# The attention's bias table by one product of rounded numbers, its operands stacked over 97 rows, and its product moved from the k projection to the v projection

## The chip, the cores and the metric

The kernel runs on one core of a Trainium2 chip. The metric is the device time of one launch in microseconds; lower is better. The median of three runs of the kernel before is 672.82 us (672.76 to 673.3).

## The reference, cut to what matters

One decoder block works on 512 tokens of width 1024. Its first half computes `q | k | v | p | g_attn | g_pool = h @ W_in`, a causal attention with 8 heads of 64, a pooling mixer, and a gated merge; its second half is a feed-forward block with a causal convolution. The change touches the additive bias of the attention's logits alone:

```
bias_t = rel_bias.T                                      # (8 heads, 32 buckets)
dist   = q_pos - k_pos
logit  = (q . k) * 64**-0.5 + bias_t[:, t5_bucket(dist)]
logit  = where(dist >= 0, logit, -inf)
prob   = softmax(logit)
```

The bias depends on the head and the distance only, so a table of 8 heads by 640 distances holds all of it. Distances below zero (the masked keys) are a 33rd bucket with the value -1e30.

## The kernel before, in words

All matrix products work on numbers split in two: `hi` is the value rounded to TensorE's short format (fp32r), by ScalarE's copy, and `lo` is the rest, by a VectorE subtraction. A product is then three fp32r matmuls (`mm3`: hi*hi, hi*lo, lo*hi). The order of TensorE, VectorE and ScalarE is the order in which the program is written (`manual_schedule`); the DMA queues of SyncE (loads of weights) and GpSimd take theirs in the written order as well.

The projections of q, k and v accumulate over 8 slices of the contraction into four PSUM banks of 128 tokens each. q and p (the pooling mixer's input) come first. k follows as a generator: `fill(kgen, us)` writes out as many pieces of it (three matmuls, counted as 0.65) as fit, and other steps are written between the fills. v does the same with `vgen`. PSUM has 8 banks, handed out in turn: k lies in the four banks that p left, and the next banks asked for are those that q left, freed one by one by q's norm (`head_norm`, VectorE, four instructions, one for each bank).

The steps that the prediction names, in the written order:

- `pooling(0)`, `pooling(1)`: VectorE sums windows of p, then a split.
- `head_norm(qps, qr, "q")`: frees q's four banks.
- `pooling(2)`: VectorE sums in a row, then ScalarE's rounding `pool_h` and VectorE's rest `pool_l`.
- `bias_table()`: for the 512 and the 128 last distances one float32 matmul of a 0/-1 matrix `hot` (33 buckets by distances) with the table `rel` (33 buckets by 8 heads) into the banks `fp_0`, `fp_1`; ScalarE copies the result to `f_0`, `f_1`; GpSimd's queue writes both to the DRAM buffer `fd`. As `fp` asks for two banks, it takes q's first two.
- `pool_proj(0)`, `pool_proj(1)`: three matmuls each into the banks `pw_0`, `pw_1`, then ScalarE's `pl_h` and VectorE's `pl_l`, which frees the bank.
- `head_sums(kps, "k")` and `head_norm(kps, kr, "k")`: squares on ScalarE, sums on VectorE, a power on GpSimd (`hr_k`), the norm on VectorE (`n_k`), which frees k's banks.
- `stacks`: transposes of q and k (`T_True`, `T_False`) and their splits into `Q`, `K1` and `kz`.
- `logits(h)`: GpSimd's queue reads row h of `fd` back, each partition shifted by one element (`trev`); TensorE computes the logits into banks `S`; VectorE adds `trev` to them and takes the minimum (line 454).
- Behind the attention, for j in 0 to 7, the branches: the products `B` (pool) and `A` (attention) with the weights `br`, whose parts are `hi_br` (ScalarE) and `lo_br` (VectorE).

`load_unit` puts a weight load on SyncE's queue in one of five buffers, `ahead` makes its hi and lo parts two units before they are needed.

Of the kernel before, what the change touches and what calls it, by code (L numbers as in the profile page):

```python
# [7 lines left out]
F32 = mybir.dt.float32  # L8
F32R = mybir.dt.float32r
AF = mybir.ActivationFunctionType  # L10
# [8 lines left out]
H = 8  # L19
# [4 lines left out]
NB = 32  # L24
EPS = 1e-6
WINDOWS = (2, 4, 8, 16)
BIG = 1e30
NF = 640
NG = 16
AW = D + 2  # L30
FIRST = 5.2
# [20 lines left out]
def block_kernel(tc, x, cvec, ada, wtok, wch, pool_w, wbr, wout, wup, wdn, pack, table, out):  # L52
    nc = tc.nc
# [3 lines left out]
    with ctx:  # L57
# [11 lines left out]
        def slot(name, dt=F32, w=512):  # L69
            return sp.tile([P, w], dt, tag="s", name=name)  # L70

        def bank(name):
            return psp.tile([P, 512], F32, tag="b", name=name)
# [11 lines left out]
        plan += [(wtok[8 + i], f"v{i}") for i in range(4)]  # L85
        plan += [(wch[i], f"gate{i}") for i in range(NG)]
        for j in range(8):
            if 8 + j >= NG:
                plan.append((wch[8 + j], f"gate{8 + j}"))
# [117 lines left out]

        fd = dpool.tile([H, NF], F32, name="fd")

        def bias_table():  # L210
            for i, (c0, n) in enumerate(((0, 512), (512, NF - 512))):
                fp = bank(f"fp_{i}")
                nc.tensor.matmul(fp[:H, :n], rb_[: NB + 1, :H], hot[i][: NB + 1, :n], start=True, stop=True)
                nc.scalar.activation(fsb[i][:H, :n], fp[:H, :n], AF.Copy)
                nc.gpsimd.dma_start(fd[:, c0 : c0 + n], fsb[i][:H, :n])

# [92 lines left out]
        for k in range(KT):  # L309
            i = k // 2  # L310
            if k % 2 == 0:
                pw, qw = ready.pop(f"p{i}"), ready.pop(f"q{i}")
            c0 = (k % 2) * 512
# [15 lines left out]
            mm3s([(qps[t], hh[k][:, tslice(t)], hl[k][:, tslice(t)], qw[0][:, ws], qw[1][:, ws])  # L329
                  for t in range(TT)], k == 0, k == KT - 1, late=1)  # L330

        hot = [slot("hot_0"), slot("hot_1")]
        rb_ = slot("rel")
        fsb = [slot("f_0"), slot("f_1")]
        nc.sync.dma_start(rb_[: NB + 1, :H], table[:, NF:])
        for i, (c0, n) in enumerate(((0, 512), (512, NF - 512))):
            nc.sync.dma_start(hot[i][: NB + 1, :n], table[:, c0 : c0 + n])

        def tok_proj(i, ps, name):
            for kk in range(4):  # L340
                w = unit(f"{name}{kk}")
                for s in range(2):
                    k = 2 * kk + s
                    for t in range(TT):
                        mm3(ps[t], hh[k][:, tslice(t)], hl[k][:, tslice(t)],
                            w[0][:, s * 512 : s * 512 + 512], w[1][:, s * 512 : s * 512 + 512],
                            k == 0, k == KT - 1)
                        yield 0.65

        def gate_proj(i, store, name):  # L350
            w = unit(name)
            ps = bank(f"{name}_ps")
            for k in range(KT):
                mm3(ps, w[0][:, tslice(k)], w[1][:, tslice(k)], hh[k], hl[k], k == 0, k == KT - 1)
                yield 0.65
            g = slot(name)
            nc.scalar.activation(g, ps, AF.Copy)
            store[i] = g

        def fill(gen, us):  # L360
            while us > 0:
                c = next(gen, None)
                if c is None:
                    return
                us -= c
# [15 lines left out]
        def head_norm(ps, rss, name):  # L381
            res = []
            for t in range(TT):
                o = slot(f"n_{name}_{t}")
                nc.vector.tensor_tensor(
                    o.rearrange("p (h d) -> p h d", d=64), ps[t].rearrange("p (h d) -> p h d", d=64),
                    rss[t].unsqueeze(2).to_broadcast([P, H, 64]), op=ALU.mult)
                res.append(o)
            return res
# [13 lines left out]
        def stacks(pr, isq):  # L403
            src, gain = (qn, qgn) if isq else (kn, col(C_KG))
            tp = bank(f"T_{pr}_{isq}")
            for t in range(TT):
                nc.tensor.transpose(tp[:, tslice(t)], src[t][:, tslice(pr)], ident)
            for e in range(2):
                h = 2 * pr + e
                a = slice(e * 64, e * 64 + 64)  # L410
                b = slice(64 - e * 64, 128 - e * 64)
                if isq:
                    q = slot(f"Q_{h}", F32R)
                    nc.scalar.activation(q[a], tp[a], AF.Copy, scale=gain[a])
                    nc.vector.scalar_tensor_tensor(
                        q[b], tp[a], gain[a], q[a].bitcast(F32), op0=ALU.mult, op1=ALU.subtract)
                    Q[h] = q
                else:
                    k1 = slot(f"K1_{h}", F32R)
                    k2 = kz[e, pr % 2]  # L420
                    for r in (a, b):
                        nc.scalar.activation(k1[r], tp[a], AF.Copy, scale=gain[a])
                    nc.vector.scalar_tensor_tensor(
                        k2[a], tp[a], gain[a], k1[a].bitcast(F32), op0=ALU.mult, op1=ALU.subtract)
                    K1[h], K2[h] = k1, k2
# [123 lines left out]
        kgen = tok_proj(1, kps, "k")  # L549
# [8 lines left out]
        pooling(1)  # L558
        fill(kgen, 4)
        qn = head_norm(qps, qr, "q")  # L560
        fill(kgen, 4)
        pooling(2)
        fill(kgen, 1)
        bias_table()
        fill(kgen, 1)
        for g in range(2):
            pool_proj(g)
        fill(kgen, 3)
# [8 lines left out]
        fill(vgen, 4)  # L577
        kn = head_norm(kps, kr, "k")
        fill(vgen, 1)
        stacks(0, True)  # L580
        fill(vgen, 2)
        stacks(1, True)
# [20 lines left out]
        def gate_stream():  # L603
            for i in range(NG):
                yield from gate_proj(i, gates, f"gate{i}")

        gg = gate_stream()
        fill(gg, FIRST)
        share = (NG * 5.2 - FIRST) / H
        for h in range(H):  # L610
# [346 lines left out]
def _bucket(d):  # L957
    if d < 16:
        return d
    return min(31, 16 + int(math.log(d / 16) / math.log(8.0) * 16))  # L960


def _layout(a):
    f = {k: np.asarray(v) for k, v in a.items()}
    one = lambda k: f[k][0]
    c = np.ascontiguousarray
    arr = {}
    arr["x"] = c(f["x"][0])
    arr["cvec"] = c(f["c"])
    unit = np.zeros((6, D, 1), np.float32)  # L970
    unit[[1, 4]] = 1.0
    arr["ada"] = c(np.concatenate(
        [one("ada_w").T, one("ada_b")[:, None], unit.reshape(6 * D, 1)], axis=1)).reshape(48, P, AW)
    w = one("w_in")
    tok = w[:, :2048].reshape(4, 2, P, 4, 512)
    arr["wtok"] = c(tok.transpose(3, 0, 2, 1, 4)).reshape(16, P, 1024)
    ch = lambda m, kt: m.reshape(kt, P, -1, P).transpose(2, 1, 0, 3)
    arr["wch"] = c(ch(w[:, 2048:], KT)).reshape(16, P, 1024)
    arr["pool_w"] = c(one("pool_w").transpose(1, 0, 2)).reshape(P, 512)
    wa, wb = ch(one("w_branch_attn"), 4), ch(one("w_branch_pool"), 4)  # L980
    arr["wbr"] = c(np.concatenate([wa, wb], axis=2)).reshape(8, P, 1024)
    tokm = lambda m: c(m.reshape(m.shape[0] // 256, 2, P, 2, 512).transpose(0, 3, 2, 1, 4)).reshape(-1, P, 1024)
    arr["wout"] = tokm(one("w_out"))
    up = ch(one("w_up"), KT).reshape(2, NP, P, 1024)
    arr["wup"] = c(up.transpose(1, 0, 2, 3)).reshape(2 * NP, P, 1024)
    dn = one("w_down").reshape(NP // 2, 2, P, 2, 512)
    blocks = np.stack([dn[:, 0, :, 0], dn[:, 0, :, 1], dn[:, 1, :, 1], dn[:, 1, :, 0]])
    blocks = np.concatenate([blocks, np.zeros((4, 2 * NU - NP // 2, P, 512), np.float32)], axis=1)
    arr["wdn"] = c(blocks.reshape(4, NU, 2, P, 512).transpose(0, 1, 3, 2, 4)).reshape(4, NU, P, 1024)
    cols = lambda v: v.reshape(-1, P).T  # L990
    qk = lambda k: np.concatenate([one(k), one(k)])[:, None]
    inv = np.zeros((P, 64), np.float32)
    for g, wd in enumerate(WINDOWS):
        inv[:, 16 * g : 16 * g + 16] = 1.0 / np.minimum(np.arange(16) + 1, wd)
    cw = one("conv_w").reshape(3, 2 * NP, P).transpose(2, 1, 0).reshape(P, -1)
    arr["pack"] = c(np.concatenate(
        [cols(one("norm1_g")), cols(one("norm2_g")), qk("q_norm_g"), qk("k_norm_g"),
         cols(one("pool_scale")), inv, np.eye(P, dtype=np.float32), cw, cols(one("conv_b"))], axis=1))
    hot = np.zeros((NB + 1, NF), np.float32)
    for i in range(NF):  # L1000
        hot[NB if i < 127 else _bucket(i - 127), i] = -1.0
    rb = np.concatenate([f["rel_bias"], np.full((1, H), -BIG, np.float32)], axis=0)
    arr["table"] = c(np.concatenate([hot, rb], axis=1))
    return arr


# [20 lines left out]
```

## Time and the profile before

| | |
|---|---|
| median of three runs | 672.82 us |
| the profiled execution's own time | 672.42 us |
| its span in the trace | 670.6 us |
| TensorE busy | 659.7 us (98%) |
| VectorE busy | 516.9 us (77%) |
| ScalarE busy | 331.7 us (49%) |
| mean granted clock of TensorE | 0.999 |

The span runs from the first to the last recorded instruction; the profiled execution's own time is 1.8 us longer, and 0.40 us below the median of the three runs. Times in the trace count from the span's start. Busy time is the time in which an engine has at least one instruction under way.

### The profile page before, as it was taken

The numbers are of one execution on the slowest core, as the hardware profiler recorded it, in microseconds if no ns is written. First come the engines' busy times: TensorE is split into PE (matmuls) and PEld (weight loads), VectorE is DVE, ScalarE is ACT, GpSimd is POOL, SyncE is SP. The second block draws the span as 40 slices with busy tenths as digits, with TensorE's granted clock in tenths as the row PEclk, the third lists the DMA queues.
The fourth block names the chain that finished last, engine by engine and source line by source line (L and its number), as shares of the span: only waits on it lengthen the run. The fifth ranks groups of instructions, "written<-read, shape, count | busy, mean of one in ns | idle before, by whom it ended". The sixth has DMA issues, their size and how long they took to land.

```text
span 670.6 us, 8750 instructions
## 1 busy us (share of the span) xinstructions
PE 659.7 (98%) x3090; PEld 549.5 (82%) x3090; DVE 516.9 (77%) x854; ACT 331.7 (49%) x532; POOL 93.3 (14%) x125
## 2 busy tenths in 40 slices
PE   6999999999999999999999999999999999999997
PEld 4788788888888887888998888888888888888885
DVE  5795776888878588867578878878787878878774
ACT  6554347756665556504653443425343344767431
POOL 3002140000000054703011111120110001001000
PEclk9999999999999999999999999999999999999999
DMA  8885231355443396693267675966935447767751
GB/s 307 294 349 186 90 128 64 114 173 190 153 145 106 103 201 217 223 351 131 95 220 253 223 247 195 307 229 215 309 127 188 162 153 148 271 224 263 254 179 58
DMA packets 41889, 131.48 MB, mean 196 GB/s; under 512 B 5379, under 2 KB 5548, under 8 KB 41846
## 3 DMA queue, kind: packets, MB, share of 16 engines
q1 hardware_dynamic: 35270, 109.82, 48.7%
q0 software_dynamic: 6576, 21.12, 9.5%
q8 instruction: 24, 0.39, 0.3%
q14 instruction: 19, 0.16, 0.1%
HBM read 115.16 MB, written 15.76 MB: 195 GB/s over the span
## 4 chain that ended last, share of the span: by engine, by line
PE 92%; DVE 2%; DMA 2%; ACT 2%; issue 1%; SPq 0%; DVEq 0%; ACTq 0%
PE u L129 12%; PE u L130 12%; PE u L128 12%; PE gate_ps L128 4%; PE gate_ps L130 4%; PE gate_ps L129 4%; PE X L893 3%; PE X L892 3%; PE X L894 3%; PE p L138 2%; PE o L130 2%; PE o L128 2%; PE q L138 2%; PE o L129 2%; PE O L495 2%; PE Y L893 1%
## 5 line engine op out<-in xcount | busy, mean ns | idle before, releaser
L128 PE MATMUL u<-h2h,hi_up 128*128 128x512 f32 (+1 forms) x384 | 142.7, 372 | 0.0
L129 PE MATMUL u<-h2l,hi_up 128*128 128x512 f32 (+1 forms) x384 | 142.6, 371 | 0.0
L130 PE MATMUL u<-h2h,lo_up 128*128 128x512 f32 (+1 forms) x384 | 142.6, 371 | 0.0
L128 PEld LDWEIGHTS u<-h2h,hi_up 128*128 128x128 f32 x384 | 72.4, 188 | 12.6
L129 PEld LDWEIGHTS u<-h2l,hi_up 128*128 128x128 f32 x384 | 72.4, 188 | 12.5
L130 PEld LDWEIGHTS u<-h2h,lo_up 128*128 128x128 f32 x384 | 72.4, 188 | 12.3
L191 DVE CUSTOM_DVE_ANT_0 raw_ada<-raw_ada,cbc 128x1026 f32<-128x1026 f32 x48 | 59.0, 1250 | 5.5 <-issue 2.7
L762 ACT ACTIVATE uv<-u,pk 128x512 f32<-128x512 f32 x22 | 17.2, 780 | 85.8 <-PE u L130 85.8
L119 DVE TENSOR_TENSOR lo_up<-raw_up,hi_up 128x1024 fp32r<-128x1024 f32 x44 | 52.0, 1219 | 4.8 <-ACT hi_up L109 4.8
L128 PE MATMUL gate_ps<-h_h,hi_gate 128*128 128x512 f32 x128 | 50.0, 391 | 0.0
L130 PE MATMUL gate_ps<-h_h,lo_gate 128*128 128x512 f32 x128 | 50.0, 390 | 0.0
L129 PE MATMUL gate_ps<-h_l,hi_gate 128*128 128x512 f32 x128 | 49.9, 390 | 0.0
L109 ACT ACTIVATE hi_up<-raw_up 128x1024 fp32r<-128x1024 f32 x44 | 44.2, 1048 | 4.3 <-PE u L129 4.3
L815 POOL DMA_DIRECT2D tsum_t<-b x44 | 23.8, 541 | 145.1 <-DVE b L810 139.0
L763 DVE SCALAR_TENSOR_TENSOR uv<-u,pk,uv 128x511 f32<-128x511 f32 x22 | 16.5, 749 | 34.2 <-ACT uv L762 34.2
L119 DVE TENSOR_TENSOR lo_t<-raw_t,hi_t 128x1024 fp32r<-128x1024 f32 (+1 forms) x24 | 26.7, 1133 | 9.6 <-ACT hi_t L109 9.6
L762 ACT ACTIVATE ug<-u,pk 128x512 f32<-128x512 f32 x22 | 17.0, 774 | 32.1 <-PE u L130 32.1
L109 ACT ACTIVATE hi_t<-raw_t 128x1024 fp32r<-128x1024 f32 (+1 forms) x24 | 23.7, 988 | 17.9 <-PE Y L894 8.8
L204 POOL TENSOR_TENSOR wo_l<-raw_wo,wo_h 128x512 fp32r<-128x512 f32 x16 | 25.6, 1620 | 20.7 <-ACT wo_h L203 20.7
L130 PEld LDWEIGHTS gate_ps<-h_h,lo_gate 128*128 128x128 f32 x128 | 24.0, 188 | 5.1
L128 PEld LDWEIGHTS gate_ps<-h_h,hi_gate 128*128 128x128 f32 x128 | 24.0, 188 | 4.6
L129 PEld LDWEIGHTS gate_ps<-h_l,hi_gate 128*128 128x128 f32 x128 | 24.0, 188 | 4.5
(253 smaller groups left out, 1507.4 us busy)
## 6 DMA issues: line engine op xcount, KB each, us to landing
raw_ada<-in_ada SPq DMA_DIRECT2D x48, 513.0 KB, 5.2
raw_up<-in_wup SPq DMA_DIRECT2D x44, 512.0 KB, 4.6
b<-in_wdn SPq DMA_DIRECT2D x44, 256.0 KB, 5.8
tsum_t<-b POOLq DMA_DIRECT2D x44, 256.0 KB, 2.9
raw_t<-tsum_t SPq DMA_DIRECT2D x20, 512.0 KB, 4.7
raw_gate<-in_wch SPq DMA_DIRECT2D x16, 512.0 KB, 3.4
raw_b<-in_wdn SPq DMA_DIRECT2D x15, 512.0 KB, 3.9
raw_br<-in_wbr SPq DMA_DIRECT2D x8, 512.0 KB, 4.3
```

The source lines that it names most:

```text
L109: nc.scalar.activation(hi, raw, AF.Copy)
L119: nc.vector.tensor_sub(lo, raw, hi.bitcast(F32))
L128: nc.tensor.matmul(ps, sh, mh, start=start, stop=False)
L129: nc.tensor.matmul(ps, sh, ml, start=False, stop=False)
L130: nc.tensor.matmul(ps, sl, mh, start=False, stop=stop)
L138: nc.tensor.matmul(ps, sl if i else sh, mh if i else ml, start=False, stop=stop and i != late)
L191: nc.vector.tensor_tensor_reduce(out=raw, in0=raw, in1=cbc, op0=ALU.mult, op1=ALU.add, scale=1.0, scalar=0.0, accum_out=acol[:, i : i + 1])
L204: (eng or nc.vector).tensor_sub(lo[:, :w], src, hi[:, :w].bitcast(F32))
L762: nc.scalar.activation(t, ps, AF.Identity, scale=cw(2), bias=col(C_CB + i))
L815: nc.gpsimd.dma_start(tsum[n, i][:, u * 512 : u * 512 + 512], b[nm])
L892: nc.tensor.matmul(ps, sh, mh, start=start, stop=False, skip_group_check=True)
L893: nc.tensor.matmul(ps, sh, ml, start=False, stop=False, skip_group_check=True)
```

## The change

The 0/-1 matrix and the table are stored twice, one below the other: rows 0 to 32 and rows 64 to 96, with zeros between (97 rows). The matrix is loaded as `hotr` and rounded to fp32r by VectorE (`hot`; 0 and -1 stay exact). The table is loaded as `rel`; ScalarE rounds all 97 rows to `rels`, then VectorE puts the rest of the rounding in rows 64 to 96. One fp32r matmul over 97 rows gives hi and lo part together. The operands are made behind q's norm, and `bias_table()` moves from between the fills of k to behind the norm of k, among the fills of v, just ahead of the first transposes.

```diff
+NT = 64 + NB + 1
...
         def bias_table():
             for i, (c0, n) in enumerate(((0, 512), (512, NF - 512))):
                 fp = bank(f"fp_{i}")
-                nc.tensor.matmul(fp[:H, :n], rb_[: NB + 1, :H], hot[i][: NB + 1, :n], start=True, stop=True)
+                nc.tensor.matmul(fp[:H, :n], rbs[:NT, :H], hot[i][:NT, :n], start=True, stop=True)
...
-        hot = [slot("hot_0"), slot("hot_1")]
+        hot = [slot("hot_0", F32R), slot("hot_1", F32R)]
+        hotr = [slot("hotr_0"), slot("hotr_1")]
+        rbs = slot("rels", F32R)
         rb_ = slot("rel")
         fsb = [slot("f_0"), slot("f_1")]
-        nc.sync.dma_start(rb_[: NB + 1, :H], table[:, NF:])
+        nc.sync.dma_start(rb_[:NT, :H], table[:, NF:])
         for i, (c0, n) in enumerate(((0, 512), (512, NF - 512))):
-            nc.sync.dma_start(hot[i][: NB + 1, :n], table[:, c0 : c0 + n])
+            nc.sync.dma_start(hotr[i][:NT, :n], table[:, c0 : c0 + n])
...
         qn = head_norm(qps, qr, "q")
+        nc.scalar.activation(rbs[:NT, :H], rb_[:NT, :H], AF.Copy)
+        nc.vector.tensor_sub(rbs[64:NT, :H], rb_[64:NT, :H], rbs[64:NT, :H].bitcast(F32))
+        for i, n in enumerate((512, NF - 512)):
+            nc.vector.tensor_copy(hot[i][:NT, :n], hotr[i][:NT, :n])
         fill(kgen, 4)
         pooling(2)
-        fill(kgen, 1)
-        bias_table()
-        fill(kgen, 1)
+        fill(kgen, 2)
...
         fill(vgen, 1)
+        bias_table()
         stacks(0, True)
...
-    arr["table"] = c(np.concatenate([hot, rb], axis=1))
+    tab = np.concatenate([hot, rb], axis=1)
+    arr["table"] = c(np.concatenate([tab, np.zeros((64 - NB - 1, NF + H), np.float32), tab], axis=0))
```

On TensorE the two products stood among the k projection's matmuls (a name's first number counts the bank, its last one the buffer):

```order
L129 MATMUL k_2_646<-lo_k2_655,h_5_h_439 128x512
L130 MATMUL k_2_646<-hi_k2_653,h_5_l_440 128x512
L213 MATMUL fp_0_793<-hot_0_588,rel_590 8x512
L213 MATMUL fp_1_797<-hot_1_589,rel_590 8x128
L128 MATMUL k_3_647<-hi_k2_653,h_5_h_439 128x512
L129 MATMUL k_3_647<-lo_k2_655,h_5_h_439 128x512
```

and now stand among those of v, ahead of the first transposes of q:

```order
L130 MATMUL v_1_878<-lo_v1_807,h_3_h_357 128x512
L131 MATMUL v_1_878<-hi_v1_805,h_3_l_358 128x512
L214 MATMUL fp_0_943<-hot_0_588,rels_592 8x512
L214 MATMUL fp_1_947<-hot_1_589,rels_592 8x128
L411 MATMUL T_0_True_951<-pk_104,n_q_0_737 128x128
L411 MATMUL T_0_True_951<-pk_104,n_q_1_739 128x128
L411 MATMUL T_0_True_951<-pk_104,n_q_2_741 128x128
```

The products left their place between two pieces of k, whose matmuls now follow each other, and moved 75 matmuls down. On VectorE, between the last norm of q and the rest of v's first weights, three instructions are new; before:

```order
L385 TENSOR_TENSOR n_q_2_738<-q_2_292,hr_q_2_635 128x512
L385 TENSOR_TENSOR n_q_3_740<-q_3_293,hr_q_3_642 128x512
L119 TENSOR_TENSOR lo_v0_752<-raw_v0_748,hi_v0_750 128x1024
L520 TENSOR_TENSOR pd_2_1_769<-pt_2_612 128x511
L521 COPY pd_2_1_769<-pt_2_612 128x1
```

and now:

```order
L389 TENSOR_TENSOR n_q_3_743<-q_3_293,hr_q_3_645 128x512
L566 TENSOR_TENSOR rels_592<-rel_593,rels_592 33x8
L568 CAST hot_0_588<-hotr_0_590 97x512
L568 CAST hot_1_589<-hotr_1_591 97x128
L120 TENSOR_TENSOR lo_v0_759<-raw_v0_755,hi_v0_757 128x1024
L524 TENSOR_TENSOR pd_2_1_776<-pt_2_615 128x511
L525 COPY pd_2_1_776<-pt_2_615 128x1
```

Everything behind them on VectorE keeps its order (`lo_v0` and then `pooling(2)` come next) and starts behind three more instructions. On ScalarE the two copies `f` left their place between the rounding `pool_h` and that of v's second weights `hi_v1`; before:

```order
L203 ACTIVATE pool_2_h_783<-pool_2_778 128x512
L214 ACTIVATE f_0_591<-fp_0_793 8x512
L214 ACTIVATE f_1_592<-fp_1_797 8x128
L109 ACTIVATE hi_v1_806<-raw_v1_804 128x1024
L536 ACTIVATE pl_0_h_817<-pw_0_813,pk_104 128x512
```

and now:

```order
L565 ACTIVATE rels_592<-rel_593 97x8
L110 ACTIVATE hi_v0_757<-raw_v0_755 128x1024
L204 ACTIVATE pool_2_h_790<-pool_2_785 128x512
L110 ACTIVATE hi_v1_805<-raw_v1_803 128x1024
L540 ACTIVATE pl_0_h_816<-pw_0_812,pk_104 128x512
```

So `hi_v1` follows `pool_h` directly, and the rounding `rels` is new ahead of `hi_v0`. The banks go round by two as well: `pw_0` and `pw_1` take q's first two banks in place of `fp`, v takes q's other two and then those of `pw_0` and `pw_1`, and `fp`, now asked for behind v, takes the first two banks of k.

## Rows read from the trace of the kernel before

**Rows 1.** The page, part 4: shares of the chain that ended last, by engine.

```profile
PE 92%; DVE 2%; DMA 2%; ACT 2%; issue 1%; SPq 0%; DVEq 0%; ACTq 0%
```

**Rows 2.** TensorE's waits, first and last of five: total, times, longest (us).

```profile
PE cb L230 <- ACT crow L150: 3.4, 1, 3.4
...
PE B L130 <- DVE lo_br L119: 0.5, 1, 0.5
```

**Rows 3.** Timeline of TensorE, 76 to 87: start, duration (us), engine, line, operation.

```profile
76.52 0.39 PE L130 MATMUL k<-hi_k,h_l 128*128 128x512 f32 x1
76.83 1.24 PE L213 MATMUL fp<-hot,rel 33*8 33x512 f32 x4
78.00 0.50 PE L128 MATMUL k<-hi_k,h_h 128*128 128x512 f32 x1
...
78.81 0.40 PE L128 MATMUL k<-hi_k,h_h 128*128 128x512 f32 x1
...
86.98 0.39 PE L128 MATMUL v<-hi_v,h_h 128*128 128x512 f32 x1
```

**Rows 4.** Weight loads (PEld) of the table's product, same columns, idle time in brackets.

```profile
76.83 0.09 PEld L213 LDWEIGHTS fp<-hot,rel 33*8 33x8 f32 x2 [0.35 <-DVE n_q L385]
```

**Rows 5.** The tile fp: minimum, median and longest duration (ns) of its matmuls.

```profile
L213 PE MATMUL fp<-hot,rel x4: 269/429/593, 76.8 to 77.8; 33*8 33x512 f32 x2, 33*8 33x128 f32 x2
```

**Rows 6.** Timeline of VectorE and ScalarE, 74 to 87.

```profile
74.60 2.48 DVE L385 TENSOR_TENSOR n_q<-q,hr_q 128x512 f32<-128x512 f32 x4
...
81.12 0.16 DVE L526 TENSOR_TENSOR fx<-pd,pk 128x8 f32<-128x8 f32 x1
...
81.52 0.63 ACT L203 ACTIVATE pool_h<-pool 128x512 fp32r<-128x512 f32 x1 [7.14 <-DVE pool L527]
...
82.06 0.73 ACT L214 ACTIVATE f<-fp 8x512 f32<-8x512 f32 x2
...
82.69 1.04 ACT L109 ACTIVATE hi_v<-raw_v 128x1024 fp32r<-128x1024 f32 x1
...
83.77 1.23 DVE L119 TENSOR_TENSOR lo_v<-raw_v,hi_v 128x1024 fp32r<-128x1024 f32 x1 [0.89 <-PE k L130]
...
84.91 1.40 DVE L537 SCALAR_TENSOR_TENSOR pl_l<-pw,pk,pl_h 128x512 fp32r<-128x512 f32 x2
...
85.57 0.74 DVE L537 SCALAR_TENSOR_TENSOR pl_l<-pw,pk,pl_h 128x512 fp32r<-128x512 f32 x1
```

**Rows 7.** VectorE's copy to fp32r, by form: count, busy us, mean ns, idle.

```profile
L107 DVE CAST hi_p<-raw_p 128x1024 fp32r<-128x1024 f32 x1 | 0.7, 689 | 0.0
```

**Rows 8.** Timeline of VectorE at 111: a short operation on one tensor.

```profile
111.19 0.29 DVE L468 TENSOR_SCALAR L<-L,ri 128x128 f32<-128x128 f32 x1
```

**Rows 9.** Timeline of VectorE and TensorE, 91 to 96.

```profile
91.72 1.87 DVE L385 TENSOR_TENSOR n_k<-k,hr_k 128x512 f32<-128x512 f32 x3
...
95.14 0.60 PE L407 MATMUL T_True<-pk,n_q 128*128 128x128 f32 x4
```

**Rows 10.** The tile f: issues of its writes to fd (ns), and their landing (us).

```profile
L215 POOL DMA_DIRECT2D fd<-f x2: 508/548/587, 82.9 to 83.5; - x2
...
DMA to landing us min/median/max: 1.5/1.7/1.9
```

**Rows 11.** The tile trev, 90 to 125: three reads of fd, issue to landing.

```profile
DMA to landing us min/median/max: 3.9/4.0/5.7
```

**Rows 12.** Timeline of VectorE at 107: the first use of trev.

```profile
107.77 0.69 DVE L454 CUSTOM_DVE_ANT_0 L<-S,trev 128x512 f32<-128x512 f32 x1
```

**Rows 13.** The chain that ended last, in order of time: two of its pieces.

```profile
229.31 0.60 ACT bot L502
...
240.68 8.61 DMA raw_ada<-in_ada
```

**Rows 14.** Timeline of TensorE at 263.

```profile
263.04 0.50 PE L130 MATMUL B<-pl_h,lo_br 128*128 128x512 f32 x1 [0.53 <-DVE lo_br L119]
```

**Rows 15.** The page, part 6: the loads of ada, KB each, median us to landing.

```profile
raw_ada<-in_ada SPq DMA_DIRECT2D x48, 513.0 KB, 5.2
```

## The prediction, as it was made before the run

> **What bounds the kernel now.** I read the page first, then TensorE's waits, then the timeline around the table's product, and last the rows of the other engines around the two places that the change touches. The chain that ended last lies on TensorE for 92% of the span [rows 1], and TensorE waits for another engine only five times in all [rows 2]. Four of those waits lie ahead of the projections or at their first matmuls; the fifth is 0.5 us in the branch stage, for VectorE's `lo_br`. From the projections on TensorE is a queue without gaps, apart from that one: a microsecond taken out of its work is one off the end, and a microsecond of new waiting is one on it. VectorE, ScalarE and the transfers count only where they make TensorE wait.
>
> In the timeline the regular step of TensorE is 0.227 us for a matmul of 512 columns: from 78.81 to 86.98 there are 36 of them in 8.17 us [rows 3].
>
> **What the change removes.** From the k matmul at 76.52 to the one at 78.81 there are four regular matmuls (0.91 us) and the table's product, in 2.29 us [rows 3]. So the float32 product costs 1.38 us in its old place. Of this its columns explain most: the four records differ by 593 - 269 = 324 ns for 384 columns more [rows 5], 0.84 ns for a column against 0.227 us / 512 = 0.44 for a regular one; twice 640 columns at 0.84 ns are 1.08 us. The other 0.30 us is a fixed price of the block: its first weights are loaded at 76.83 and not under the matmul ahead of it, with 0.35 us of idle time before [rows 4], and the regular matmul behind it takes 0.50 us instead of 0.39 and its followers come late [rows 3]. The idle time is put down to q's norm, but that is not what is waited for: the banks asked for are those of the first two of four `n_q`, and the whole row of four ends at 77.08 [rows 6], so the second was through by about 75.9. The whole 1.38 us therefore goes with the product.
>
> **What it adds on TensorE.** One fp32r pass over 640 columns is 640 x 0.44 ns = 0.28 us: that is the lower bound, if nothing else is paid. The upper bound has the 0.30 us of the old block once more: 0.58. The nearest row is the old product itself, which gives 8 rows of output as the new one does, so I take 0.58. The row that decides is [rows 4], where the small product's weights wait for the matmul ahead. The Trainium skill (TensorEngine Tiling (Array Packing), Key Properties) says that a change of the tiling mode, not only of the tile, drains TensorE; an output of 8 rows would be such a change in its old shape and in its new one, and the trace's 0.30 us for entering and leaving agrees with a drain that doesn't care for the number format. By that rule the new product costs the 0.58, without it the 0.28.
>
> **What it adds on VectorE, and who waits for it.** Three instructions now stand behind q's norm. The subtraction over 8 columns is like `fx`, 0.16 us [rows 6]. For the two copies to fp32r the trace has one of 1024 columns, 0.689 us [rows 7]; 640 columns in proportion are 0.43 us, the lower bound. The upper one takes a short operation's 0.29 us for 128 columns [rows 8] and a straight line from there to 0.689 for the 512: 0.46, together 0.75. So VectorE is later by 0.59 to 0.91 us; I take 0.75. ScalarE's rounding of 8 columns stands ahead of `hi_v0`, which VectorE needs only behind q's norm, so it is covered.
>
> What is queued behind is `lo_v0` and the whole of `pooling(2)`, then, through ScalarE, `hi_v1`, `lo_v1`, and the two `pl_l` that free the banks `pw_0` and `pw_1`. Before, ScalarE had `pool_h` at 81.52, the two copies `f` at 82.06 (0.73 us), and `hi_v1` from 82.69 for 1.04 us; `lo_v1` began 0.04 us behind its end, at 83.77 [rows 6]. (The row names a matmul of k as what ended that wait, but it ends with `hi_v1`.) Now the copies `f` are gone from there, and `hi_v1` follows `pool_h` directly: it begins at 82.06 + 0.75 = 82.81 instead of 82.69. Nearly all the VectorE time is covered by the 0.63 us that `f` held ScalarE, and `lo_v1` and what follows are 0.12 us later than before (-0.04 to +0.28 at the bounds).
>
> TensorE, though, comes 1.38 us earlier. The third bank of v is that of `pw_0`. v's first matmul into it is the 36th behind the one at 78.81 (three of k from there, six of `pw`, 21 of k, six of v); it stood at 86.98 [rows 3], and now at 85.60. The first `pl_l` ran from 84.91 for 0.74 us, to 85.65 [rows 6], now to 85.77. Before, the bank was free 1.33 us ahead of time; now it is 0.17 us late. With 0.04 us for the signal, and with a matmul behind a wait taking 0.50 instead of 0.39 us [rows 3, 14], TensorE loses 0.32 us here. At the lower bound the bank is free at 85.61, just when it is wanted, and I count nothing; at the upper one 0.48 us. I take 0.3. The second `pl_l`, 0.66 us later, meets a matmul that is 0.68 us later plus the same wait, and costs nothing more.
>
> **What moves at no cost.** The new place of the product asks for k's first two banks, the transposes `T_True` behind it for the third. Three `n_k` run from 91.72 for 1.87 us, to 93.59 [rows 9], now to about 93.7. TensorE was at the transposes at 95.14 [rows 9], so it comes to the product at 95.14 - 1.38 + 0.32 = 94.08: 0.37 us behind even the third norm. If that cover went, each microsecond of `n_k` would be one on the end. The writes to `fd` move with the product: it ends at 94.66, ScalarE's copies take 0.73 us, the two issues 1.1 us and the landing 1.9 us at most [rows 6, 10], so `fd` is there at about 98.4; the first `trev` takes up to 5.7 us [rows 11], to 104.1. VectorE adds it at 107.77 [rows 12], now about 0.5 us earlier, so about 3 us are left. Behind the writes on GpSimd's queue stand only the reads `trev`. The table's load grows from 33 to 97 partitions on SyncE's queue at 50 us, ahead of v's weights and of others that are used 20 us later; its cover is these 20 us.
>
> **The sum.** -1.38 + 0.58 + 0.30 = -0.50 us. Against the profiled execution's own time that is 672.42 - 0.50 = 671.92 us; the median of the runs stands 0.40 us above that execution, so I predict 672.3 us. By the bounds the gain is 0.32 to 1.10 us, 672.5 to 671.7 us. What a measurement of this kernel can tell from no change is about 0.2%, or 1.35 us: even the best case is within it.
>
> **The rivals.** *No wait at v's third bank.* If VectorE's three instructions cost their lower bound or hide better, nothing is lost there, and the gain is 0.8 us (with the product at 0.58) to 1.10 us (at 0.28): 671.7 to 672.0 us. For it: 0.17 us is less than I know the copies' time to. Against: the bank would still come at the very moment it is wanted.
>
> *The gain is given back in the branch stage.* From 229.31 on the chain that ended last leaves TensorE for ScalarE, VectorE and one transfer of `ada` of 8.61 us [rows 13], and returns with TensorE's wait of 0.53 us at 263.04 [rows 14]. There TensorE has no reserve. If the end of that chain is set by the transfers and not by TensorE's last attention product at 229.31, TensorE comes 0.5 us earlier and waits 0.5 us longer: 672.8 us. For it: a wait that exists already. Against it: the chain starts from a TensorE matmul, so it ought to move along.
>
> *Slower.* At that same place the load of `ada` that took 8.61 us, where the median of 48 is 5.2 [rows 15], lands later still, because it now meets the other transfers at another moment. Each microsecond there is one on the end. The kernel is slower than before from 0.5 us more, and by over 0.2% from 1.9 us more (10.5 us in all). The load has already spread by 8.61 - 5.2 = 3.4 us to the slow side; half as much again, 1.7 us, gives 674.0 us, the whole of it once more 675.7. Against it: the order of the loads is unchanged and they move together.
>
> **How the numbers follow.** My forecast has 0.55, no wait at v 0.20, the gain given back 0.11, slower 0.06; 0.08 is left for a gain of more than 1.35 us, which no row here supports. The range takes the bounds of the sum (671.7 to 672.5), the case that gives all back (672.8), and 0.2 us on either side for the spread of the three runs (672.76 to 673.3): 671.6 to 673.0 us. Faster by over 0.2%: 0.08; within: 0.86; slower by over 0.2%: 0.06.
>
> **What the profile after would show.** The k matmuls run on at 76.7 us in steps of 0.227. Two matmul records of the table stand at about 94, 0.28 us of columns and about 0.3 us around them. TensorE's list of waits has a new entry, v behind `pl_l`, of about 0.2 us at 85.6; if it is missing, the first rival holds. VectorE has 0.6 to 0.9 us of new work behind `n_q`, and `hi_v1` directly behind `pool_h`. The wait for `lo_br` near 262.5 stays at about 0.5 us; at 1 us the gain was given back there, at 2.5 us or more the kernel is slower. The prediction would be wrong, beyond these, if `trev` landed later than about 107, or if the product had to wait for k's norm at 94.

## The result: slower by 3.87 us, where 0.5 us less was predicted

The changed kernel takes 676.66 us (median of four runs, 676.18 to 677.0) against 672.79 us for the kernel before in the same runs: a ratio of 1.0055, 95% interval 1.0043 to 1.0066. The prediction (672.3 us, range 671.6 to 673.0) is wrong in sign and size. The profiled execution took 676.18 us, its span is 674.4 us, the granted clock 0.999 as before.

The page, part 4, of the changed kernel, answers to [rows 1]. TensorE's share of the chain that ended last is down from 92 to 83%; VectorE has 6% where it had 2, and transfers 4% where they had 2:

```profile
PE 83%; DVE 6%; DMA 4%; ACT 3%; issue 2%; SPq 1%; POOL 0%; DVEq 0%; ACTq 0%
```

TensorE's waits after (total, times, longest in us), the answer to [rows 2]; four others, ahead of the projections or at their first matmuls, are left out:

```profile
PE v L129 <- DVE pl_l L541: 2.7, 1, 2.7
...
PE k L130 <- DVE lo_k L120: 0.8, 1, 0.8
...
PE k L129 <- ACT hi_k L110: 0.4, 1, 0.4
PE B L131 <- DVE lo_br L120: 0.4, 1, 0.4
```

Three of these are new. One, v behind `pl_l`, was forecast at 0.2 us; it is 2.7. Two stand in k, of which the prediction says that it runs on without a gap. The wait for `lo_br` is 0.4 where it was 0.5. The same three in TensorE's timeline after (start, duration in us, engine, line, operation; idle time before it in brackets), with the new product; this answers to [rows 3, 9]:

```profile
77.47 0.39 PE L131 MATMUL k<-hi_k,h_l 128*128 128x512 f32 x1
78.27 0.50 PE L129 MATMUL k<-hi_k,h_h 128*128 128x512 f32 x1 [0.41 <-ACT hi_k L110]
79.53 0.50 PE L130 MATMUL k<-lo_k,h_h 128*128 128x512 f32 x1 [0.76 <-DVE lo_k L120]
...
87.52 0.39 PE L131 MATMUL v<-hi_v,h_l 128*128 128x512 f32 x1
90.65 0.50 PE L129 MATMUL v<-hi_v,h_h 128*128 128x512 f32 x1 [2.74 <-DVE pl_l L541]
...
98.73 0.39 PE L131 MATMUL v<-hi_v,h_l 128*128 128x512 f32 x1
98.95 0.45 PE L214 MATMUL fp<-hot,rels 97*8 97x512 f32 x2
99.24 0.60 PE L411 MATMUL T_True<-pk,n_q 128*128 128x128 f32 x4
```

Measured by the distance of two starts less the regular 0.227, the two waits in k cost 0.57 and 1.03 us, the slow steps behind them 0.28, and the wait in v 2.90 with 0.14 behind it: 4.92 us. From the first matmul of k to the first of the gate projection the kernel took 49.62 us before,

```profile
61.10 0.39 PE L128 MATMUL k<-hi_k,h_h 128*128 128x512 f32 x1
...
110.72 0.39 PE L128 MATMUL gate_ps<-h_h,hi_gate 128*128 128x512 f32 x1
```

and 53.43 after, 3.81 more:

```profile
61.38 0.39 PE L129 MATMUL k<-hi_k,h_h 128*128 128x512 f32 x1
...
114.81 0.39 PE L129 MATMUL gate_ps<-h_h,hi_gate 128*128 128x512 f32 x1
```

The old product's 1.38 us went and the new one's 0.29 came: 4.92 - 1.38 + 0.29 = 3.83. So the whole loss lies in this stretch, and it is waiting.

What is late? The chain that ended last, after, in order of time (start, duration in us, what):

```profile
54.97 5.11 SPq L78
...
61.42 8.30 DMA pwr<-in_pool_w
...
89.93 0.67 DVE pl_l L541
90.65 0.50 PE v L129
```

Ahead of v's late matmul it doesn't lie on TensorE. It runs through SyncE's queue, where the issue of v's weights (line 78) is on the path, through the load of the pooling weights `pwr` and ScalarE's rounding `pwh` into VectorE's work, which reaches TensorE as `pl_l`. The timeline of SyncE's queue, before:

```profile
50.49 0.72 SPq L337 DMA_DIRECT2D hot<-in_table  x2
51.31 3.43 SPq L77 DMA_DIRECT2D raw_v<-in_wtok  x3
54.80 0.43 SPq L552 DMA_DIRECT2D pwr<-in_pool_w  x1
```

and after:

```profile
50.68 3.48 SPq L341 DMA_DIRECT2D hotr<-in_table  x2
54.26 7.11 SPq L78 DMA_DIRECT2D raw_v<-in_wtok  x3
61.42 0.52 SPq L556 DMA_DIRECT2D pwr<-in_pool_w  x1
```

The two issues of the table take 3.48 us in place of 0.72, the three of v's weights 7.11 in place of 3.43. `pwr` is issued 6.6 us later, and lands 8.3 us behind its issue where it took 5.8. What the transfers did meanwhile is read from windows of one microsecond (the last two columns are the mean busy share of the 16 DMA engines and GB/s), before:

```profile
54.00:55.00 1.00, 1.00 (x7) 0.81 (x6) 0.46 (x2) 0.00 (x0) 0.00 (x0) 1.00 1.04 352
```

and after:

```profile
54.00:55.00 1.00, 1.00 (x6) 0.84 (x5) 0.96 (x2) 0.00 (x0) 0.00 (x0) 1.00 0.07 25
...
57.00:58.00 1.00, 1.00 (x7) 0.81 (x6) 0.00 (x0) 0.00 (x0) 0.00 (x0) 1.00 0.07 27
```

0.07 of sixteen engines is one engine, at 25 to 27 GB/s (so in five of the six windows from 54 to 60). The matrix of 97 x 640 numbers of 4 bytes is 248 KB, some 9.5 us at that rate, and the queue's next transfers stand behind it. The records of single packets in the trace, which no view above prints, show the same: the 97 rows of 512 columns (2048 bytes each) go one at a time, 0.08 us apart, from 54.08 to 61.82, and with the table's other two parts the load lasts from 53.5 to 64.7 us, 11.2 us, where the 33 rows took 1.7 us before. ScalarE at `pwh` shows the result: it sat idle for 5.84 us, and the rounding begins at 69.74, where it began at 63.50 before.

```profile
69.74 0.63 ACT L558 ACTIVATE pwh<-pwr 128x512 fp32r<-128x512 f32 x1 [5.84 <-DMA pwr<-in_pool_w]
```

From `pwl` at 70.41 VectorE works almost without a gap through the pooling, k's `lo_k`, q's norm (from 79.39; 74.60 before, [rows 6]) and the new copies to `pl_l`: 4.8 us late at q's norm, and 4.9 at the first `pl_l`.

### The profile page after: what moved, and what is told of

The parts are those of the page before. It is cut to its first block, busy times and chain, and to the rows that moved or that the text cites. A ratio compares the mean times of both kernels' runs of the same rounds, so it can differ in the third digit from the quotient of the medians.

```text
span 674.4 us, 8751 instructions
## 1 busy us (share of the span) xinstructions
PE 659.5 (98%) x3088; PEld 549.0 (81%) x3088; DVE 517.5 (77%) x857; ACT 331.5 (49%) x533; POOL 93.1 (14%) x125
## 4 chain that ended last, share of the span: by engine, by line
PE 83%; DVE 6%; DMA 4%; ACT 3%; issue 2%; SPq 1%; POOL 0%; DVEq 0%; ACTq 0%
PE u L131 12%; PE u L130 12%; PE u L129 12%; PE gate_ps L131 4%; PE gate_ps L130 4%; PE gate_ps L129 4%; PE X L900 3%; PE X L901 3%; PE X L899 3%; PE o L129 2%; PE o L131 2%; PE o L130 2%; DVE raw_ada L192 2%; PE O L499 2%; PE Y L900 1%
```

## The experiments

Three theories of the loss. **A:** the 97 rows go through one DMA engine, 97 being a prime number, and `pool_w`, behind them on the queue, is late. **B:** it is the bytes, three times as many as for 33 rows. **C:** it is the new place of the product and VectorE's three new instructions. In the runs of the experiments the kernel before had medians of 674.61 to 675.02 us, so ratios are compared, and for the stretch "k to gate" (first matmul of k to first of the gate projection) the trace of the kernel before taken among them (e9): 49.66 us. Two traces of one kernel differ by less than 0.1 us in this stretch (49.62 and 49.66, 53.43 and 53.51 of the changed kernel). The ratios differ from what it shows by up to 0.9 us (e11; more in e3, whose trace is of a long run), so gains of this size are read from the stretch, and a ratio counts where its interval leaves 1 out.

**e1: the load in two parts, rows 0 to 95 and row 96.**

```diff
-        nc.sync.dma_start(rb_[:NT, :H], table[:, NF:])
-        for i, (c0, n) in enumerate(((0, 512), (512, NF - 512))):
-            nc.sync.dma_start(hotr[i][:NT, :n], table[:, c0 : c0 + n])
+        for r in (slice(0, 96), slice(96, NT)):
+            nc.sync.dma_start(rb_[r, :H], table[r, NF:])
+            for i, (c0, n) in enumerate(((0, 512), (512, NF - 512))):
+                nc.sync.dma_start(hotr[i][r, :n], table[r, c0 : c0 + n])
```

> Theory A (one engine): the load of 97 rows runs on one DMA engine alone, at the 25 to 27 GB/s that the changed kernel's windows show from 54 to 60 us; what is queued behind it on SyncE, pool_w among it, comes 6.6 us late, and with it ScalarE's pwh and all of VectorE's chain up to the banks that v needs. Here the same bytes and values come as 96 rows and one row. A expects pool_w issued near 56, pwh as early as in the kernel before, no wait of k for its third and fourth weights, a wait of v of 0.4 us or less, and 671.9 us (671.6 to 672.4). Theory B (bytes): three times the bytes on the queue are what delays pool_w; it expects 676 to 677 us as in the changed kernel. Theory C (place and VectorE's three instructions): the load is innocent; it expects 676 to 677 us too. The Trainium skill (DMA: Bandwidth & Descriptors, Why a DMA increments its semaphore by 16 and not by 1) says that a load is dealt to the largest number of engines up to 16 that divides its rows: 1 for 97, 16 for 96, 11 for the 33 of before.

Measured: 674.19 us against 674.66, ratio 0.9995 (0.9986 to 1.0004); k to gate 48.93 us. SyncE's queue:

```profile
52.07 0.88 SPq L342 DMA_DIRECT2D hotr<-in_table  x2
...
53.33 0.54 SPq L342 DMA_DIRECT2D hotr<-in_table  x2
...
57.19 1.51 SPq L557 DMA_DIRECT2D pwr<-in_pool_w  x1
```

The same bytes in more instructions, and the loss is gone, with the waits in k. (The time is not shown to be below that of the kernel before: the interval holds 1, and A had expected 671.9 us of 672.8 before, 0.9987.) What remains is the wait at v that was forecast: the matmul comes at 87.03 and not at 86.51 + 0.227, and its slower follower adds 0.11, 0.40 us together. Its weight load:

```profile
87.03 0.19 PEld L129 LDWEIGHTS v<-hi_v,h_h 128*128 128x128 f32 x1 [0.56 <-DVE pl_l L542]
```

**e2: the kernel before with nothing but the load of 97 rows.** The product stays in float32, 33 rows, in its old place.

```diff
...
-        nc.sync.dma_start(rb_[: NB + 1, :H], table[:, NF:])
+        nc.sync.dma_start(rb_[:NT, :H], table[:, NF:])
         for i, (c0, n) in enumerate(((0, 512), (512, NF - 512))):
-            nc.sync.dma_start(hot[i][: NB + 1, :n], table[:, c0 : c0 + n])
+            nc.sync.dma_start(hot[i][:NT, :n], table[:, c0 : c0 + n])
...
```

> The kernel before, with nothing changed but the table's load: 97 rows (rows 33 to 96 are loaded and not used). Theory A (one engine) expects the delay of pool_w and of VectorE's chain as in the changed kernel, with the product still in its old place: 675 to 676.7 us. Theory B (bytes) expects the same here. Theory C (place and VectorE's three instructions) expects no change, 672.8 us.

Measured: 678.30 us, ratio 1.0054 (1.0042 to 1.0066); k to gate 54.13 us. The queue reads like that of the changed kernel:

```profile
51.36 2.92 SPq L338 DMA_DIRECT2D hot<-in_table  x2
54.38 7.11 SPq L78 DMA_DIRECT2D raw_v<-in_wtok  x3
61.54 0.48 SPq L553 DMA_DIRECT2D pwr<-in_pool_w  x1
```

The load alone loses what the whole change loses, so C falls. (In the stretch it loses 4.47 us, about the change's 3.81 and the 0.7 that the change gains there without the slow load, by e1.) TensorE meets the late VectorE at another place, the old product, which waits 2.8 us for q's norm to free its banks:

```profile
PE fp L214 <- DVE n_q L386: 2.8, 1, 2.8
```

**e3 and e5: the changed kernel, with the table padded by zeros to 106 rows (2 x 53) and to 99 (9 x 11).** Only the load is longer; the product keeps its 97 rows.

```diff
+NR = 106
...
-            nc.sync.dma_start(hotr[i][:NT, :n], table[:, c0 : c0 + n])
+            nc.sync.dma_start(hotr[i][:NR, :n], table[:, c0 : c0 + n])
...
```

> The changed kernel with a table padded by nine rows of zeros to 106, all loaded: 9 per cent more bytes, and a number of rows that two engines can share. Theory A (one engine), with the engine count of the Trainium skill's rule (2 for 106), expects the load to last about half as long, 5 us, pool_w some 2 us late instead of 6.6, and 672.2 to 673.2 us. Theory B (bytes) expects 676.5 us or more. Theory C (place and VectorE's instructions) expects 676 to 677 us.

> The changed kernel with a table padded by two rows of zeros to 99, all loaded: more rows and bytes than the 97 that cost 3.9 us, but a number that 11 engines can share, as the 33 of before. Theory A (one engine) expects SyncE's issue of pool_w near 56.5 us, no late pwh, a wait of v of 0.3 us and a time like that of the split into 96 rows and one: 0.3 to 0.7 us below the kernel before, ratio 0.9990 to 0.9997. Theory B (bytes) expects a ratio of 1.005 or more; half of the delay (1.002) would mean that both count.

Measured: 106 rows 675.27 us, ratio 1.0012 (1.0001 to 1.0023), k to gate 52.54 us in the profiled run, which is one of the longer of its twelve (676.68 us); 99 rows 673.54 us, ratio 0.9984 (0.9974 to 0.9995), k to gate 48.90. The queue with 106 rows, and then with 99:

```profile
51.30 1.34 SPq L342 DMA_DIRECT2D hotr<-in_table  x2
...
57.31 0.42 SPq L557 DMA_DIRECT2D pwr<-in_pool_w  x1
```

```profile
51.27 0.74 SPq L342 DMA_DIRECT2D hotr<-in_table  x2
...
55.59 2.73 SPq L557 DMA_DIRECT2D pwr<-in_pool_w  x1
```

Two more rows than 97 and the loss is gone; nine more and part of it is back, with `pwr` landing 9.8 us behind its issue and a wait of 2.1 us at v. (A had expected 672.2 to 673.2 us of it; on that scale the ratio makes it 673.6.) Bytes can't do that, so B falls. In the windows from 54 to 58, where the changed kernel moved mostly 25 to 27 GB/s, the one with 99 rows moves 291 to 352:

```profile
54.00:55.00 1.00, 1.00 (x6) 0.84 (x5) 1.00 (x2) 0.00 (x0) 0.00 (x0) 1.00 0.91 291
```

The packet records show how many rows are under way at once. One row of 2048 bytes takes 0.08 us; within this time one starts with 97 rows, two at most with 106, and up to ten with 99. The whole load takes 11.2, 8.6 and 1.9 us. The Trainium skill (DMA: Bandwidth & Descriptors, Why a DMA increments its semaphore by 16 and not by 1) says that a transfer uses the largest number of engines up to 16 that divides its slowest dimension: by that rule 33 rows use 11, 97 one, 96 sixteen, 106 two and 99 eleven. The order of these runs agrees with it, and so do the rows under way at once: one, two, and up to ten, with which eleven engines agree.

**e4: the load of 97 rows as it is, issued behind that of `pool_w`.**

> The changed kernel with the load of 97 rows issued behind pool_w's on SyncE, not ahead of v's first weights. Theory A (one engine), in the form that the late pool_w is what costs the time, expects pwh as early as before and 671.7 to 672.4 us, although the load still takes 9 us on one engine. Theory B (bytes) expects the same if pool_w is the victim. If v's weights, which are blocked too, were the victims and not pool_w, v's fourth weights would now come late and TensorE would wait for them: 673 us or more. Theory C (place and VectorE's instructions) expects 676 to 677 us.

Measured: 674.01 us, ratio 0.9992 (0.9981 to 1.0003); k to gate 49.00 us.

```profile
56.51 1.20 SPq L553 DMA_DIRECT2D pwr<-in_pool_w  x1
...
58.08 3.43 SPq L556 DMA_DIRECT2D hotr<-in_table  x2
```

The load is as slow as in the changed kernel (3.43 us for its two issues) and costs nothing, since nothing that is needed soon stands behind it. In this run the first three of v's weights, too, are ahead of the load. That `pool_w` is the victim and not they is read from the trace of the changed kernel: no engine waits there for one of v's weights, though they land up to 12.3 us behind their issue, and ScalarE waits 5.84 us for `pwr`.

**e6 and e7: one part of the change without the other.** e6 has the new operands and the load in two parts, with the product in its old place; e7 moves the old float32 product of 33 rows to its place beside v.

> The short format alone: table loaded as 96 rows and one, operands behind q's norm, but the product in its old place between the fills of k. TensorE saves 1.38 us and pays 0.29 us for the new product, as the changed kernel's trace has it. The copies f stay on ScalarE ahead of hi_v1, so VectorE's 0.67 us of new work reach the two pl_l in full: the first ends at 86.3, v's first matmul into its bank would come at 85.9, a wait of 0.5 to 0.6 us with its restart. Expected 0.5 us below the kernel before (ratio 0.9993). The rival, that VectorE's work is hidden, expects 1.1 us below (0.9984).

> The move alone: the float32 product over 33 rows as before, loaded as before, but beside v ahead of the first transposes. It costs 1.1 to 1.4 us there as in its old place, VectorE has no new work, and ScalarE's copies f no longer stand ahead of hi_v1, so the pl_l are early and v does not wait. Expected 0 to 0.3 us below the kernel before (ratio 0.9996 to 1.0000). The rival, that the new place itself costs time (k's norm, the writes to fd, trev), expects it slower by 0.5 us or more.

Measured: e6 674.68 us, ratio 1.0006 (0.9993 to 1.0018), k to gate 49.75; e7 674.01 us, 0.9995 (0.9986 to 1.0005), 49.53. In e6 the product waits at its old place for its own operands:

```profile
77.78 0.45 PE L214 MATMUL fp<-hot,rels 97*8 97x512 f32 x2 [0.97 <-DVE hot L569]
```

The gain of 1.1 us turns into a wait of 0.97 and the steps behind it. That wait I had not foreseen here; the wait of v that I expected in its place doesn't come. In e7 the float32 product is as dear beside v as it was in k:

```profile
93.69 0.39 PE L130 MATMUL v<-hi_v,h_l 128*128 128x512 f32 x1
94.01 1.24 PE L213 MATMUL fp<-hot,rel 33*8 33x512 f32 x4
95.18 0.66 PE L407 MATMUL T_True<-pk,n_q 128*128 128x128 f32 x4
```

95.18 - 93.69 less one regular step is 1.26 us, and its transposes take 0.06 us longer than those behind the new product. So in the stretch the move alone gains 0.13 us and the new product alone nothing (-0.09), and the two together 0.7 (e1).

**e8 and e11: the operands made behind `pooling(2)`,** which keeps VectorE's three instructions out of the way of `pool_l` and `hi_v1`; e8 with the load in two parts, e11 with 99 rows.

```diff
         qn = head_norm(qps, qr, "q")
+        fill(kgen, 4)
+        pooling(2)
         nc.scalar.activation(rbs[:NT, :H], rb_[:NT, :H], AF.Copy)
...
-        fill(kgen, 4)
-        pooling(2)
         fill(kgen, 2)
```

> The changed kernel with the table loaded as 96 rows and one, and the operands made behind pooling(2) and not behind q's norm. There VectorE sits idle for hi_v1 in any case (0.26 us in the runs with the split load, 0.89 us before), so the first pl_l ends near 85.4 on the scale of the kernel before, ahead of v's matmul at 85.6. Expected: no wait of v, TensorE 1.09 us shorter up to the gates, 1.1 us below the kernel before (ratio 0.9984), 0.4 us below the split load alone. The rival, that a gain of that size is lost in the branch stage, expects the ratio of the split load, 0.9995, with a longer wait for the parts of br.

> The changed kernel with the table padded to 99 rows and the operands made behind the last pooling step: the two mends of the earlier runs in one, with one load for each part. From the first k matmul to the gate 48.5 us, as with the load in two parts and the same place (48.55). Ratio to before 0.998 to 0.9995. If the 99 rows had a merit of their own beyond being spread over more engines, it would be below 0.998.

Measured: e8 673.26 us, ratio 0.9990 (0.9981 to 0.9998), k to gate 48.55 us; e11 673.12 us against 675.02, ratio 0.9971 (0.9960 to 0.9982), 48.57 us. In e8 v's third bank comes in time, one regular step behind the matmul ahead:

```profile
85.43 0.39 PE L131 MATMUL v<-hi_v,h_l 128*128 128x512 f32 x1
85.66 0.42 PE L129 MATMUL v<-hi_v,h_h 128*128 128x512 f32 x1
```

Both beat the kernel before, and with it the changed one. The traces show 1.1 us for each in the stretch, as expected for e8, whose ratio amounts to 0.7 us; that e11's ratio amounts to 1.9 us is not found in them, and it stays open whether 99 rows have a merit of their own.

**e9 and e10: the kernel before and the changed one, unchanged, for their traces among the others.** The eight experiments ahead of these all show a second wait in the branch stage, for `hi_br`.

> The kernel before, unchanged, to have its trace from the same runs as the experiments. Two theories of the branch stage: the first eight experiments all show a second wait of TensorE there, for hi_br, of 0.6 to 0.8 us, which neither of the two first traces has. (P) it belongs to the chip and the run, whatever the kernel: then this trace shows it too, and B to o takes 45.3 to 46.2 us, not 44.5. (Q) it comes from having less work ahead of the branches, and gives the gain back: then this trace shows 44.5 us and one wait of 0.5 us. From the first k matmul to the gate 49.6 us by both.

> The changed kernel, unchanged, for the same reason. From the first k matmul to the gate 53.4 us, as in its first trace. (P) B to o 45.3 to 46.2 us with a wait for hi_br of 0.6 to 0.8 us; (Q) 44.2 us and one wait of 0.4 us, since here nothing was gained ahead of the branches.

Measured: 674.09 us (e9) and 679.81 us (e10), one run each; k to gate 49.66 and 53.51 us; from the first `B` to the first `o` 45.82 and 46.19 us, where the first traces had 44.54 and 44.23. TensorE's waits of e9, and then of e10:

```profile
PE B L128 <- ACT hi_br L109: 0.8, 1, 0.8
```

```profile
PE B L129 <- ACT hi_br L110: 0.8, 1, 0.8
```

Both kernels have the wait, so (P) holds: it belongs to the chip or the run and is no giving back of a gain. In the experiments the stretch takes 45.3 to 46.2 us, around e9's 45.8. Of the 5.72 us between these two single runs 3.85 lie in the stretch from k to the gate; 0.37 are in the branch stage, and the rest was not followed.

## Why the prediction was wrong

**The step that failed** is in the part on what moves at no cost: "The table's load grows from 33 to 97 partitions on SyncE's queue at 50 us, ahead of v's weights and of others that are used 20 us later; its cover is these 20 us." It was priced at nothing, and no rival had it. Two things in it are wrong. No duration was worked out for the load: it takes 11.2 us where it took 1.7, and not for its bytes but for its number of rows (e5 against the changed kernel). And "others that are used 20 us later" hid one that is used much sooner: `pwr` was issued at 54.80, landed 5.8 us later, at 60.6, and `pwh` read it at 63.50, so its reserve was 2.9 us and not 20. Both rows were in the trace of before (the tile `pwr`; ScalarE's timeline):

```profile
DMA to landing us min/median/max: 5.8/5.8/5.8
...
63.50 0.65 ACT L554 ACTIVATE pwh<-pwr 128x512 fp32r<-128x512 f32 x1
```

VectorE took up `pwh` only at 65.60, 1.4 us behind the end of the rounding, so up to VectorE the reserve was about 4.3 us. After, `pwr` landed 9.1 us later, at 69.7, and VectorE is late by what is left, 4.8 us (70.41 for 65.60). Had `pool_w` been named there, a rival with a slower load would have had a condition (more than these 4.3 us) and a victim (VectorE's queue). Undoing this step alone (e1) brings the kernel back to 0.9995, and doing it alone (e2) gives 1.0054.

**The other steps**, judged in e1, where the load is out of the way:

- *The old product* went with its 1.38 us: k runs in regular steps there.
- *The new product* was priced at 0.58 us, between a lower bound of 0.28 and that upper one. It costs 0.29 (98.95 to 99.24 after). The weight loads that stood out in [rows 4] no longer do: the first lies ahead of the product, under the matmul before it (the row below). The fixed price came with the float32 product of 33 rows, in either place (in e7 0.24 us above its 1.08 of columns), not with this one. By the rule of the Trainium skill that I set beside it (TensorEngine Tiling (Array Packing), Key Properties), that a change of the tiling mode drains TensorE, it ought to have cost 0.58, if 8 rows of output are such a change. No drain is seen here, and the runs don't tell whether the mode changes.

```profile
L214 PEld LDWEIGHTS fp<-hot,rels x2: 88/89/90, 98.7 to 99.0; 97*8 97x8 f32 x2
```

- *VectorE's three instructions* took 0.67 us, 81.90 to 82.57 after, where I took 0.75 from 0.59 to 0.91 (first start, duration, operation):

```profile
81.90 0.17 DVE L566 TENSOR_TENSOR rels<-rel,rels 33x8 fp32r<-33x8 f32 x1
82.09 0.56 DVE L568 CAST hot<-hotr 97x512 fp32r<-97x512 f32 x2
82.57 1.22 DVE L120 TENSOR_TENSOR lo_v<-raw_v,hi_v 128x1024 fp32r<-128x1024 f32 x1
```

- *The wait at v's third bank* was right in place and cause: 0.40 us in e1 where 0.32 was worked out. e8 takes it away by the order of VectorE's work alone.
- *The sum* by these measured terms is -1.38 + 0.29 + 0.40 = -0.69 us; e1 shows 48.93 - 49.66 = -0.73 in the stretch. That my -0.50 is near it is in part luck: the product was priced 0.29 too dear and the wait 0.10 too cheap.
- *The writes and reads of `fd`*, and k's norm, cost nothing, as said: `trev` landed 5.5 us behind its issue at most, and the product follows v's matmul after a regular step.

**The rivals.** "No wait at v's third bank" was not so: with the operands where the change puts them, v waits even without the load's delay (e1). "The gain is given back in the branch stage" is not borne out: e5, e8 and e11 gain 0.8 to 1.1 us up to the gate and take 45.5 to 45.9 us in the branch stage, as the kernel before does in e9 (45.8). "Slower" had the sign, and the wrong transfer: `ada` did nothing (the wait for `lo_br` is 0.4 us), `pool_w` did it.

## What to carry to other kernels

When a load changes its shape, look at its number of rows before its bytes: 97 took one engine's rate, 99 did not. Then list every transfer behind it on its queue with three numbers from the trace, issue, landing and first use; the smallest reserve sets the price, however far off the consumer of the loaded data is. Two rows of zeros more, a load in two parts, or a later place on the queue each took the loss away here. And where a stall is found on an engine far from the load, follow the chain of waits back to the queue's issues: here v's weights, `pool_w`, its rounding and VectorE's work lie between the table and the matmul that waits.

## What was not expected of the hardware

An issue on SyncE's queue, mostly 0.33 us in the same trace, takes up to 5.81 us behind the slow load (one of the three in 7.11): the engine that issues is itself held up, so also what it would issue next. That is not the slow load's alone: with 99 rows the issue of `pool_w` took 2.73 us. With one DMA engine at work, at 25 to 27 GB/s, the other fifteen stood nearly idle for 6 us (a share of 0.06 to 0.12 from 54 to 60), while the queue's next transfers waited. And a chip or a run can add 0.8 us of waiting and 1.3 to 2 us to the branch stage in every kernel alike (e9, e10), which is more than the 0.5 us that the change was forecast to gain; only a trace of the kernel before from the same runs told this apart from a gain given back.
